# Two transformer networks in one f32 kernel: a fifth ring slot, transposed modulation sums, shifted low halves and a reordered feed-forward entry

## The chip, the cores and the metric

The kernel runs on one core of one Trainium2 chip. The metric is the device time of one execution in microseconds, as the median of the runs shown; lower is better. A profile is one such execution with the hardware profiler on.

## The reference

All tensors are f32; there are 256 tokens of width D = 2048. The first network has two layers, the second one adaLN block that takes a vector `c` of 2048 elements. Cut to what matters here:

```python
for l in range(2):                                   # first network
    proj = rmsnorm(x, norm_g[l]) @ w_in[l]           # 2048 x 7168
    y = concat([conv_branch, differential_attention, memory_attention])
    x = x + y @ w_out[l]

mod = silu(c) @ w_mod + b_mod                        # w_mod is 2048 x 12288
sh1, sc1, g1, sh2, sc2, g2 = split(mod, 6)
h = rms_norm(x, mix_norm_pre) * (1 + sc1) + sh1      # mixer
y = token_mixer(h)     # w_in_2, sliding-window attention, gated linear
                       # attention (GLA), two branch products, w_out_2
x = x + g1 * rms_norm(y, mix_norm_post)
h = rms_norm(x, ffn_norm_pre) * (1 + sc2) + sh2      # feed-forward block
u = causal_conv(h @ w_up)                            # 2048 x 11264
y = (silu(gate(u)) * val(u)) @ w_down                # 5632 x 2048
x = x + g2 * rms_norm(y, ffn_norm_post)
```

## The kernel before, in words

**Products.** Every large product is made in three passes of TensorE: an f32 operand is split into a high half (`hi`, a cast to fp32r) and a low half (`lo`, what the cast left), and the product is hi·hi + hi·lo + lo·hi. I call these three matmuls a *triple*. `gemm_as` (lines 342 to 356) and `gemm_halves` (360) hold the activations stationary and stream 512 weight columns; the rows of a triple stand in lines 354, 355 and 356. `gemm_ws` (393 to 408) holds the weights stationary and streams the 256 tokens; its lines are 406, 407 and 408. The split activations live in pairs of tiles: A (high) and B (low), or C (high) and D (low), 16 KB a partition each. `pair_AB` (1296) makes the pair A, B with the low half moved by 32 elements, 128 bytes, inside B; elsewhere A, B and C, D start where their tiles start.

**The weights' path.** The weights come as pieces of 512 KB (two tiles of 128 rows, 512 columns), in one fixed list of items. `load` (218) issues a piece on SP's queue into a slot of the ring `raw`, which has `RB` = 4 slots; `consume` (224) lets ScalarE cast it to `hi` and VectorE subtract to `lo`, into rings of `HB` = 4 slots. The load of the piece `RB` places on is issued by SP after `consume`, and waits for that slot:

```python
if j + self.RB < len(src):
    load(j + self.RB)
```

All other work (normalisations, attention, evacuations of PSUM, transposes) is written as Python generators. `run` (206) calls `tick` (278) after each piece, which advances these generators as far as a credit of VectorE and ScalarE time allows: first `evac`, then `urgent`, then background tasks. So the order on each engine is fixed when the program is built.

**The modulation.** `w_mod` has 192 pieces, which `spread_mod` (187) puts between the others: 64 in the first network, 96 in the mixer, 32 in the feed-forward block. `plan_mod` (596) turns each into two steps of VectorE, `macc = raw * c + macc`, 512 columns wide. After eight pieces `mod_done` (622) transposes `macc` in blocks of 32 and reduces it to `mred`; after four such groups a matmul with a matrix of ones sums `mred` over the partitions, and the result plus `b_mod` goes to `modT`.

**Second network.** `mixer` (1796) ends with the product with `w_out_2`; its last 512 columns run in `gemm_halves`, and `ev_last` (1931) then makes the residual rows X (`y` in the rows) of the first 128 tokens (tb 0) and the first chunk of the others (tb 1). `add_x` (1966) adds one chunk of 512 columns. `residual` (1975) does the rest chunk by chunk: `raw_chunk` (1315) transposes a chunk on TensorE, and between its steps stand the next chunk's `add_x`, the store of x and the sums of squares. `shift_norm` (1350) makes the pair C, D for the product with `w_up`; `ffn` (1998) makes the pair `gv` in A, B for the product with `w_down`, whose last 512 columns again run in `gemm_halves`.

Of the kernel before, what the change touches and what calls it, by code (L numbers as in the profile page):

```python
# [6 lines left out]
F32 = mybir.dt.float32  # L7
F32R = mybir.dt.float32r
# [3 lines left out]
ALU = mybir.AluOpType  # L12
AX = mybir.AxisListType

P = 128
# [45 lines left out]
    return [512] * (n // 512)  # L61


def row_tiles(n):

    return 16 if n == 16 else 1024 // n


def lay_pieces(np, name, w):

    layers, rows, n = w.shape
    out, c0 = np.empty((layers, rows * n), w.dtype), 0
# [81 lines left out]


class Kernel:
    RB = 4
    HB = 4
    NBG = 3
    CAP = 4.5  # L160
# [302 lines left out]
    def setup(self, ctx):  # L463
        nc, tc, a = self.nc, self.tc, self.a
        pool = lambda name, **k: ctx.enter_context(tc.tile_pool(name=name, bufs=1, **k))
        self.cp = pool("consts")
        self.wp = pool("weights")
        self.ap = pool("acts")
        dp = pool("dram", space=bass.MemoryType.DRAM)
        self.scr = {n: dp.tile(s, F32, tag=n, name=n) for n, s in (  # L470
            ("x1", [2 * P, D]), ("x2", [2 * P, D]), ("x3", [2 * P, D]), ("gp1", [D]), ("gp2", [D]))}
# [12 lines left out]
        self.mhalf = self.cp.tile([P, 16], F32, tag="mhalf", name="mhalf")  # L484
        self.cols = self.cp.tile([P, 704], F32, tag="cols", name="cols")
        self.modT = self.cp.tile([P, 96], F32, tag="modT", name="modT")
        raw = self.st["xraw"] = self.ap.tile([P, 16, 256], F32, tag="X16", name="xraw")
# [22 lines left out]
    def params(self):  # L510
# [22 lines left out]

        yield
        self.st["params"] = True

    def params_attn(self):
        nc, a = self.nc, self.a
# [56 lines left out]

    def plan_mod(self):

        nc = self.nc
        self.mod_queue = deque()
        w = self.weight("w_mod_2")  # L600
        for j in range(24):
            box = {}
            for k0 in range(0, 16, 2):
                def fn(raw, j=j, k0=k0, box=box):
                    if k0 == 0:
                        if j > 1:
                            self.await_tasks(f"red{j - 2}", bg=False)
                        box["acc"] = self.cp.tile([P, 512], F32, tag="macc", name=self.nm("macc"), bufs=2)
                    acc = box["acc"]
                    for kk in range(2):  # L610
                        s = self.ca[:, k0 + kk:k0 + kk + 1]
                        if k0 + kk == 0:
                            nc.vector.tensor_scalar(out=acc, in0=raw[:, kk], scalar1=s, scalar2=None, op0=ALU.mult)
                        else:
                            nc.vector.scalar_tensor_tensor(out=acc, in0=raw[:, kk], scalar=s, in1=acc,
                                                           op0=ALU.mult, op1=ALU.add)
                    if k0 == 14:
                        self.evac.append(self.mod_done(j, acc))
                src = w.piece(k0, 2, j * 512, 512)
                self.mod_queue.append(Item("mod", fn, src, 2, 512))  # L620

    def mod_done(self, j, acc):

        nc = self.nc
        yield
        if j % 4 == 0:
            self.mred = self.cp.tile([P, 64], F32, tag="mred", name=self.nm("mred"), bufs=2)
        red = self.mred
        while not self.t1.ok():
            yield  # L630
        for h in range(2):
            tr = self.t1.get()
            nc.vector.transpose(tr, acc[:, 256 * h:256 * h + 256])
            b = 16 * (j % 4) + 8 * h
            nc.vector.tensor_reduce(out=red[:, b:b + 8], in_=tr.rearrange("p (b i) -> p b i", i=32), axis=AX.X, op=ALU.add)
            self.t1.put(tr)
        self.st[f"red{j}"] = True
        if j % 4 < 3:
            return
        yield  # L640
        yield
        pt = self.bank()
        nc.side.matmul(pt[:, 0:64], self.cst[:, C_SUM:C_SUM + P], red, start=True, stop=True)
        for q in range(4):
            b = slice(32 * q, 32 * q + 32)
            nc.vector.tensor_tensor(out=self.modT[b, 4 * j - 12:4 * j + 4],
                                    in0=pt[b, 0:64].rearrange("p (c q) -> p q c", q=4)[:, q],
                                    in1=self.cols[b, R_BMOD + 4 * j - 12:R_BMOD + 4 * j + 4], op=ALU.add)
        self.ps.put(pt)
        for i in range(4):  # L650
            self.st[f"mod{j - i}"] = True

    def mod_row(self, gcol, postcol, dst):

# [237 lines left out]
    def layer(self, l, last):  # L892
# [137 lines left out]
        def out_begin():  # L1030
# [8 lines left out]
            if last:  # L1039
                self.await_tasks(*[f"mod{j}" for j in range(8)])  # L1040
                self.shifted("G1", R_MIXPRE, 16, 0)
                st["raw"] = [self.lp.tile([P, 4, 256], F32, tag=t, name=self.nm("raw")) for t in ("dv", "dg", "mkT", "mg")]
            else:
                st["xT2"] = [self.ap.tile([P, 16, 256], F32R, tag=t, name=self.nm(t)) for t in ("A", "B")]
# [305 lines left out]
    def shift_norm(self):  # L1350
# [15 lines left out]
        self.t1.put(dg)  # L1366
        self.ps.put(pt)
        st["r_ready"] = True
        hi, lo = [self.ap.tile([P, 16, 256], F32R, tag=t, name=self.nm(t)) for t in ("C", "D")]
# [241 lines left out]
    def gla_pair(self, c):  # L1611
# [5 lines left out]
        for hh in range(2):  # L1617
# [178 lines left out]
    def mixer(self):  # L1796
# [134 lines left out]
        def ev_last(acc):  # L1931
            c = slice(1536, 2048)
            X, ss, gp = st["X"], st["ss"], st["gp1"].pop(0)
            r = st["ry"] = self.sm.get([P, 2])
            for tb in range(2):
                rt = r[:, tb:tb + 1]
                self.square_sum(acc[tb], ss[:, tb, 3:4])
                nc.vector.tensor_reduce(out=rt, in_=ss[:, tb], axis=AX.X, op=ALU.add)
                self.rstd(rt, rt, 1.0 / D, 1)
                if tb == 0:  # L1940
                    nc.vector.tensor_tensor(out=X[:, tb, c], in0=acc[tb], in1=gp, op=ALU.mult)
                for n in range(1 if tb else 4):
                    self.add_x(n, tb)
            self.ps.put(acc[0])
            st["y"] = acc[1], gp
            yield
# [10 lines left out]
    def open_f(self):  # L1957
# [8 lines left out]
    def add_x(self, n, tb):  # L1966

        nc, st = self.nc, self.st
        xo, r = st[f"xo{n}"], st["ry"]
        x = st["X"][:, tb, n * 512:n * 512 + 512]  # L1970
        nc.vector.scalar_tensor_tensor(out=x, in0=x, scalar=r[:, tb:tb + 1], in1=xo[:, tb], op0=ALU.mult, op1=ALU.add)
        if tb:
            self.tm.put(st.pop(f"xo{n}"))

    def residual(self):
# [4 lines left out]
        for n in range(4):  # L1980
            c = slice(n * 512, n * 512 + 512)
            for i, _ in enumerate(self.raw_chunk(X[:, :, c], n, st["raw"][n])):
                if n == i == 0:
                    acc, gp = st.pop("y")
                    nc.vector.tensor_tensor(out=X[:, 1, 1536:2048], in0=acc, in1=gp, op=ALU.mult)
                    self.ps.put(acc)
                if i:
                    if n < 3:
                        self.add_x(n + 1, 1)
                    nc.sync.dma_start(out=self.scr["x3"][:, c].rearrange("(t p) d -> p t d", p=P), in_=X[:, :, c])  # L1990
                    for tb in range(2):
# [6 lines left out]
    def ffn(self):  # L1998
# [263 lines left out]
```

## Time and profile before

| | us |
|---|---|
| median of 3 runs (lowest, highest) | 2567.68 (2567.05, 2570.22) |
| the profiled execution, its own time | 2563.99 |
| its span, first to last instruction | 2562.2 |

The mean granted clock of TensorE in the profiled execution was 0.997 of full. Of the page, part 1 gives the busy time of each engine, part 5 groups of instructions, part 6 the DMA issues. Times of a stretch count from the span's start: the first network runs to 966 us, the mixer to 1710, its last output columns and the entry to the feed-forward block to 1850, then the products with `w_up` and `w_down` take turns in three parts each; the first part of `w_down` runs from 1985 to 2073 us, the second of `w_up` from 2073 to 2258. PE's waits name what TensorE waited for: `PE acc L355 <- DVE lo` is line 355 waiting for VectorE's `lo`.

### The profile page before, as it was taken

How to read it: one execution, taken by the hardware profiler on the slowest of the kernel's cores; microseconds unless marked ns; L12 is line 12 of the kernel's file. 1: busy time of each engine (PE TensorE's matmuls, PEld its weight loads, DVE VectorE, ACT ScalarE, POOL GpSimd, SP SyncE). 2: the span in 40 equal slices, each digit the busy share in tenths (PEclk: the TensorE clock that was granted, in tenths of full speed). 3: DMA queues.
4: the chain of work that ended last, by engine and by line, in shares of the span. 5: the costliest groups of instructions: out<-in, count | busy, mean ns of one | idle time of the engine just before them, and what ended most of it. 6: DMA issues, size and time to landing. Idle time of an engine off the chain costs nothing.

```text
span 2562.2 us, 38632 instructions
## 1 busy us (share of the span) xinstructions
PE 2526.8 (99%) x15079; PEld 2227.7 (87%) x15079; DVE 1823.1 (71%) x2469; ACT 1266.9 (49%) x1826; POOL 52.0 (2%) x43
## 2 busy tenths in 40 slices
PE   9999999999999999999999999999999999999998
PEld 7889998788899989878988778777999899988996
DVE  6768767786786756777777777775777667765665
ACT  6645544564554455355454334344744444543443
POOL 1000000010010000000000000000000000000000
PEclk9999999999999999999999999999999999999999
DMA  8775568887656576755558888886566766676655
GB/s 311 225 255 181 179 197 271 299 272 256 220 179 190 180 249 187 224 173 190 193 182 267 285 290 286 280 289 210 164 215 231 230 215 214 223 236 197 198 188 174
DMA packets 168903, 576.77 MB, mean 225 GB/s; under 512 B 18272, under 2 KB 24576, under 8 KB 168720
## 3 DMA queue, kind: packets, MB, share of 16 engines
q1 hardware_dynamic: 168432, 574.04, 69.0%
q8 instruction: 118, 1.93, 0.3%
q14 instruction: 65, 0.53, 0.1%
q10 hardware_dynamic: 288, 0.26, 0.0%
HBM read 565.83 MB, written 8.40 MB: 224 GB/s over the span
## 4 chain that ended last, share of the span: by engine, by line
PE 77%; DMA 9%; DVE 8%; ACT 3%; issue 2%; POOL 0%; ACTq 0%; DVEq 0%; POOLq 0%
PE acc L355 13%; PE acc L356 13%; PE acc L354 13%; PE acc L406 10%; PE acc L407 10%; PE acc L408 10%; PE pb L133 5%; DMA raw<-w_in 4%; DVE lo L133 4%; ACT hi L133 2%; DMA raw<-w_out 2%; DMA raw<-w_branch_gla 1%; DVE macc L133 1%; DMA raw<-w_branch_attn 1%; DVE tm L133 1%
## 5 line engine op out<-in xcount | busy, mean ns | idle before, releaser
L133 DVE TENSOR_TENSOR lo<-raw,hi 128x1024 fp32r<-128x1024 f32 (+1 forms) x847 | 1026.8, 1220 | 515.7 <-ACT hi L133 511.2
L133 ACT CAST hi<-raw 128x1024 fp32r<-128x1024 f32 (+1 forms) x847 | 881.7, 1048 | 867.6 <-PE acc L356 281.4
L408 PE MATMUL acc<-C,lo 128*128 128x256 f32 (+1 forms) x1424 | 403.0, 283 | 0.8 <-DVE lo L133 0.8
L406 PE MATMUL acc<-C,hi 128*128 128x256 f32 (+1 forms) x1424 | 403.7, 284 | 0.0
L407 PE MATMUL acc<-D,hi 128*128 128x256 f32 (+1 forms) x1424 | 402.9, 283 | 0.0
L354 PE MATMUL acc<-hi,C 128*128 128x512 f32 x992 | 393.1, 396 | 0.0
L355 PE MATMUL acc<-lo,C 128*128 128x512 f32 x992 | 387.4, 390 | 4.0 <-DVE lo L133 3.9
L356 PE MATMUL acc<-hi,D 128*128 128x512 f32 x992 | 387.0, 390 | 0.0
L355 PE MATMUL acc<-lo,A 128*128 128x512 f32 x904 | 357.7, 396 | 1.2 <-DVE lo L133 1.1
L356 PE MATMUL acc<-hi,B 128*128 128x512 f32 x904 | 357.9, 396 | 0.0
L354 PE MATMUL acc<-hi,A 128*128 128x512 f32 x904 | 354.2, 392 | 0.7 <-ACT hi L133 0.7
L133 DVE SCALAR_TENSOR_TENSOR macc<-raw,ca,macc 128x512 f32<-128x512 f32 x360 | 269.7, 749 | 9.9 <-DMA raw<-w_mod 2.9
L406 PEld LDWEIGHTS acc<-C,hi 128*128 128x128 f32 (+1 forms) x1424 | 271.7, 191 | 1.5 <-issue 0.7
L408 PEld LDWEIGHTS acc<-C,lo 128*128 128x128 f32 (+1 forms) x1424 | 271.7, 191 | 1.4 <-DVE lo L133 1.0
L407 PEld LDWEIGHTS acc<-D,hi 128*128 128x128 f32 (+1 forms) x1424 | 271.8, 191 | 0.6
L406 PE MATMUL acc<-A,hi 128*128 128x256 f32 x896 | 256.3, 286 | 0.0
L407 PE MATMUL acc<-B,hi 128*128 128x256 f32 x896 | 252.0, 281 | 0.0
L408 PE MATMUL acc<-A,lo 128*128 128x256 f32 x896 | 251.2, 280 | 0.3 <-DVE lo L133 0.2
L355 PEld LDWEIGHTS acc<-lo,C 128*128 128x128 f32 x992 | 186.4, 188 | 45.5 <-DVE lo L133 7.9
L354 PEld LDWEIGHTS acc<-hi,C 128*128 128x128 f32 x992 | 186.3, 188 | 40.5 <-issue 3.4
L356 PEld LDWEIGHTS acc<-hi,D 128*128 128x128 f32 x992 | 186.2, 188 | 39.3
L354 PEld LDWEIGHTS acc<-hi,A 128*128 128x128 f32 x904 | 172.7, 191 | 40.9 <-ACT hi L133 1.6
(269 smaller groups left out, 2989.5 us busy)
## 6 DMA issues: line engine op xcount, KB each, us to landing
raw<-w_in SPq DMA_DIRECT2D x406, 512.0 KB, 4.4
raw<-w_mod SPq DMA_DIRECT2D x192, 512.0 KB, 4.6
raw<-w_up SPq DMA_DIRECT2D x176, 512.0 KB, 4.2
raw<-w_out SPq DMA_DIRECT2D x96, 512.0 KB, 4.5
raw<-w_down SPq DMA_DIRECT2D x88, 512.0 KB, 4.3
raw<-w_mem_kv SPq DMA_DIRECT2D x32, 512.0 KB, 4.4
raw<-w_branch_gla SPq DMA_DIRECT2D x32, 512.0 KB, 4.7
tm<-x SPq DMA_DIRECT2D x20, 512.0 KB, 6.2
```

The costliest lines, as they stand in the source:

```text
L133: return f(*args, **kw)
L354: nc.tensor.matmul(o, xh[:, kt, t], hi, start=s, stop=False)
L355: nc.tensor.matmul(o, xh[:, kt, t], lo, start=False, stop=False)
L356: nc.tensor.matmul(o, xl[:, kt, t], hi, start=False, stop=e)
L406: nc.tensor.matmul(o, hi[:, c], xh, start=s and j % 2 == 0, stop=False, skip_group_check=True)
L407: nc.tensor.matmul(o, hi[:, c], xl, start=False, stop=False, skip_group_check=True)
L408: nc.tensor.matmul(o, lo[:, c], xh, start=False, stop=e, skip_group_check=True)
```

## The change

1. `RB` goes from 4 to 5.
2. `w_mod` is laid out transposed: a piece holds 128 output columns on the partitions and one half (1024) of the inputs along the row. One custom VectorE instruction per piece multiplies it with a broadcast row of silu(c) (`crow`, one half of 1024 at a time) and sums into `mpart` (first half) or, with `mpart` added, into `modT`. `macc`, `mred`, `mod_done` and its matmuls are gone; `b_mod` is added once in four pieces of a second half. The groups (0,8), (8,20), (20,24) set when the half changes; `crow` is broadcast six times, and a sum of the new half waits for its broadcast.
3. The low half D is allocated 64 elements longer and moved by `skew`: 0 in the mixer, 32 elements in the feed-forward block. `gv` uses `pair_AB`.
4. `ev_last` sums the squares of tb 0 itself (ScalarE) and three quarters of tb 1's sum ahead of the last, merges the last steps into one, and adds the first chunk of tb 1 in two halves of 256 columns. `residual` adds each chunk of tb 1 one step earlier, and squares tb 1 alone but in the last chunk.
5. `gla_pair` writes two gates in place of q and k (`V` tiles 6 to 4). The extra slot and the rows `crow` and `mpart` move every later tile in SBUF.

```diff
-    RB = 4
+    RB = 5
...
+        for i, (h, b) in enumerate(order):
+            def fn(raw, i=i, h=h, b=b):
+                self.await_tasks(f"crow{self.mod_half[i]}", bg=False)
+                d = raw.rearrange("p k n -> p (k n)")
+                out = self.mpart[:, b:b + 1] if h == 0 else self.modT[:, b:b + 1]
+                nc.vector.tensor_tensor_reduce(out=d, in0=d, in1=self.crow, scale=1.0,
+                                               scalar=0.0 if h == 0 else self.mpart[:, b:b + 1], op0=ALU.mult, op1=ALU.add,
+                                               accum_out=out)
...
+                if i + 1 < len(order) and self.mod_half[i + 1] != self.mod_half[i]:
+                    self.evac.append(self.crow_load(self.mod_half[i + 1]))
...
+    def crow_load(self, m):
+
+        for _ in range(2 if m else 0):
+            yield
+        h = m % 2
+        self.nc.sync.dma_start(out=self.crow, in_=self.scr["crow"][1024 * h:1024 * h + 1024].partition_broadcast(P))
+        self.st[f"crow{m}"] = True
...
+        lo = self.ap.tile([P, 16 * 256 + 64], F32R, tag="D", name=self.nm("D"))
+        s = st["skew"]
+        lo = lo[:, s:s + 4096].rearrange("p (k t) -> p k t", t=256)
...
-            Q, K, QI, KS, K2, QD = V(0), V(1), V(2), V(3), V(4, (2, P)), V(5, (2, 64))
+            Q, K, QI, KS, K2, QD = V(0), V(1), q, k, V(2, (2, P)), V(3, (2, 64))
...
+            nc.vector.tensor_reduce(out=r1, in_=ss[:, 1, 0:3], axis=AX.X, op=ALU.add)
+            nc.vector.tensor_scalar(out=r1, in0=r1, scalar1=1.0 / D, scalar2=EPS, op0=ALU.mult, op1=ALU.add)
+            for n in range(4):
+                self.add_x(n, 0)
+                if n < 3:
+                    self.square_sum(X[:, 0, n * 512:n * 512 + 512], ss[:, 0, n:n + 1])
+            self.square_sum(acc[1], ss[:, 1, 3:4])
+            nc.vector.scalar_tensor_tensor(out=r1, in0=ss[:, 1, 3:4], scalar=1.0 / D, in1=r1, op0=ALU.mult, op1=ALU.add)
+            nc.gpsimd.tensor_tensor(out=r1, in0=r1, in1=self.mhalf[:, :1], op=ALU.pow)
+            for i in range(2):
+                self.add_x(0, 1, i)
...
                 if n == i == 0:
                     acc, gp = st.pop("y")
+                    self.add_x(1, 1)
                     nc.vector.tensor_tensor(out=X[:, 1, 1536:2048], in0=acc, in1=gp, op=ALU.mult)
                     self.ps.put(acc)
+                if (n, i) in ((0, 1), (1, 0)):
+                    self.add_x(2 + n, 1)
                 if i:
-                    if n < 3:
-                        self.add_x(n + 1, 1)
                     nc.sync.dma_start(out=self.scr["x3"][:, c].rearrange("(t p) d -> p t d", p=P), in_=X[:, :, c])
-                    for tb in range(2):
+                    for tb in range(0 if n == 3 else 1, 2):
                         self.square_sum(X[:, tb, c], ss[:, tb, n:n + 1])
...
-                st["gv"] = [self.ap.tile([P, 16, 256], F32R, tag=t, name=self.nm(t)) for t in ("A", "B")]
+                st["gv"] = self.pair_AB()
```

What this does to the order on the engines, at three places. VectorE before, in the feed-forward block, around one modulation piece that ends a group of eight (`tm` are steps of the convolution, `t1k` the transposed blocks):

```order
L133 TENSOR_TENSOR lo_18289<-raw_18157,hi_18288 128x1024
L133 SCALAR_TENSOR_TENSOR macc_17168<-raw_18196,ca,macc_17168 128x512 x2
L133 TENSOR_TENSOR lo_18323<-raw_18231,hi_18322 128x1024
L133 TENSOR_TENSOR lo_18353<-raw_18261,hi_18352 128x1024
L133 STREAM_TRANSPOSE t1k_82_18383<-macc_17168 128x256
L133 TENSOR_REDUCE mred_18382<-t1k_82_18383 128x8
```

VectorE now, in the mixer near its first branch product, with three pieces (`ISA` is the custom sum, and behind it the read of the accumulator; `ml` is an evacuation):

```order
L145 ISA raw_13497,mpart<-raw_13497,crow 128x1024
L145 ISA mpart 128x1
L145 TENSOR_TENSOR lo_13586<-raw_13521,hi_13585 128x1024
L145 ISA raw_13537,modT<-raw_13537,crow,mpart 128x1024
L145 ISA modT 128x1
L145 TENSOR_TENSOR lo_13608<-raw_13543,hi_13607 128x1024
L145 TENSOR_TENSOR lo_13628<-raw_13567,hi_13627 128x1024
L145 ISA raw_13583,modT<-raw_13583,crow,mpart 128x1024
```

Per piece one long step stands between the `lo` steps where two stood, and nothing is left to do after eight pieces. SP's queue now, at the same place, where the half changes:

```order
L234 DMA raw_13537<-w_mod 128x1024
L234 DMA raw_13543<-w_branch_attn 128x1024
L234 DMA raw_13567<-w_branch_attn 128x1024
L234 DMA raw_13583<-w_mod 128x1024
L234 DMA raw_13589<-w_in 128x1024
L646 DMA crow<-crow 128x1024
L234 DMA raw_13605<-w_in 128x1024
L234 DMA raw_13611<-w_mod 128x1024
```

The broadcast has come in between the weight loads; here, as at one other of the six places, the sum that needs it is that of a piece loaded just ahead of it (`raw_13537`, the first into `modT`), and on VectorE the rows behind that sum stand behind the broadcast.

VectorE before, at the entry to the feed-forward block (`y` is X, `tm` the chunks of x, `B` the low half of `raw_chunk`):

```order
L133 TENSOR_REDUCE sm_117_16149<-sm_116_15503 128x1
L133 TENSOR_SCALAR sm_117_16149<-sm_117_16149 128x1
L133 SCALAR_TENSOR_TENSOR y_15502<-y_15502,sm_117_16149,tm_65_15528 128x512
L133 SCALAR_TENSOR_TENSOR B_16006<-pb_217_16172,G_16003,A_16005 128x256 x2
L133 TENSOR_TENSOR y_15502<-pb_216_16016,gpr_4_15853 128x512
L133 SCALAR_TENSOR_TENSOR B_16006<-pb_218_16184,G_16003,A_16005 128x256 x2
L133 SCALAR_TENSOR_TENSOR y_15502<-y_15502,sm_117_16149,tm_66_15646 128x512
```

And now:

```order
L145 SCALAR_TENSOR_TENSOR sm_117_15842<-sm_116_15209,sm_117_15842 128x1
L145 SCALAR_TENSOR_TENSOR y_15208<-y_15208,sm_117_15842,tm_65_15234 128x256 x2
L145 SCALAR_TENSOR_TENSOR B_15699<-pb_213_15870,G_15696,A_15698 128x256 x2
L145 SCALAR_TENSOR_TENSOR y_15208<-y_15208,sm_117_15842,tm_66_15350 128x512
L145 TENSOR_TENSOR y_15208<-pb_212_15709,gpr_4_15546 128x512
L145 SCALAR_TENSOR_TENSOR B_15699<-pb_214_15883,G_15696,A_15698 128x256 x2
L145 SCALAR_TENSOR_TENSOR y_15208<-y_15208,sm_117_15842,tm_67_15431 128x512
```

Two steps on the sum became one, the first chunk is added in halves, and the chunks `tm_66` and `tm_67` are added one step earlier against the `B` rows of the chunk before.

## Rows read from the trace of the kernel before

**Rows 1.** Page, part 1: busy time of each engine in the whole span

```profile
PE 2526.8 (99%) x15079; PEld 2227.7 (87%) x15079; DVE 1823.1 (71%) x2469; ACT 1266.9 (49%) x1826; POOL 52.0 (2%) x43
```

**Rows 2.** Windows by stage: length, busy time (instructions) by engine, PEclk, DMA, GB/s

```profile
0.00:966.00 966.00, 961.86 (x5698) 845.43 (x5699) 699.15 (x963) 516.06 (x803) 42.92 (x29) 1.00 0.72 231
966.00:1710.00 744.00, 732.04 (x3755) 609.11 (x3754) 563.59 (x804) 345.09 (x494) 5.44 (x9) 1.00 0.73 237
...
1710.00:1782.00 72.00, 68.67 (x296) 56.41 (x297) 41.96 (x47) 33.60 (x44) 0.28 (x1) 0.98 0.73 242
1782.00:1850.00 68.00, 61.67 (x464) 59.58 (x463) 50.70 (x90) 49.10 (x104) 1.53 (x3) 0.95 0.46 146
...
1850.00:2562.20 712.20, 702.59 (x4873) 657.14 (x4871) 467.66 (x570) 323.02 (x382) 1.84 (x2) 1.00 0.65 211
```

**Rows 3.** Waits of PE in the mixer, 966 to 1710 us: total, times, longest

```profile
PE acc L355 <- DVE lo L133: 5.9, 12, 0.9
...
PE pb L133 <- DVE tm L133: 4.2, 3, 2.1
```

**Rows 4.** Waits of PE, 1710 to 1785 us, then 1782 to 1850 us

```profile
PE pb L133 <- DVE mred L133: 3.3, 1, 3.3
...
PE pb L133 <- DVE y L133: 4.5, 2, 2.5
```

**Rows 5.** Timeline near 1443 us: start, us, engine, operation, [idle before, ended by]

```profile
1441.75 1.53 DVE L133 SCALAR_TENSOR_TENSOR macc<-raw,ca,macc 128x512 f32<-128x512 f32 x2
...
1443.83 1.05 ACT L133 CAST hi<-raw 128x1024 fp32r<-128x1024 f32 x1 [3.25 <-DMA raw<-w_in]
...
1446.19 0.50 PE L355 MATMUL acc<-lo,C 128*128 128x512 f32 x1 [0.77 <-DVE lo L133]
```

**Rows 6.** Waits of ACT in the mixer, 966 to 1710 us

```profile
ACT hi L133 <- DMA raw<-w_in: 114.9, 63, 4.1
```

**Rows 7.** DMA issues, KB each, median us to landing

```profile
raw<-w_in SPq DMA_DIRECT2D x406, 512.0 KB, 4.4
...
gpr<-gp SPq DMA_DIRECT2D x8, 256.0 KB, 5.7
```

**Rows 8.** Line 354 in three stretches: ns of one (min/median/max), first and last start

```profile
L354 PE MATMUL acc<-hi,A x128: 389/389/396, 1984.9 to 2073.0; 128*128 128x512 f32 x128
...
L354 PE MATMUL acc<-hi,C x52: 389/389/389, 121.4 to 156.0; 128*128 128x512 f32 x52
...
L354 PE MATMUL acc<-hi,A x32: 389/389/398, 1503.7 to 1524.9; 128*128 128x512 f32 x32
```

**Rows 9.** Line 406 in three stretches

```profile
L406 PE MATMUL acc<-C,hi x512: 277/283/283, 2073.7 to 2257.6; 128*128 128x256 f32 x171
...
L406 PE MATMUL acc<-A,hi x105: 274/282/469, 326.7 to 363.6; 128*128 128x256 f32 x105
...
L406 PE MATMUL acc<-A,hi x64: 278/279/282, 846.2 to 868.2; 128*128 128x256 f32 x64
```

**Rows 10.** Groups of DVE by form: busy us, mean ns | idle before

```profile
L133 DVE TENSOR_TENSOR lo<-raw,hi 128x1024 fp32r<-128x1024 f32 x842 | 1023.7, 1223 | 515.3 <-ACT hi L133 510.8
...
L133 DVE SCALAR_TENSOR_TENSOR macc<-raw,ca,macc 128x512 f32<-128x512 f32 x360 | 269.7, 749 | 9.9 <-DMA raw<-w_mod 2.9
...
L133 DVE STREAM_TRANSPOSE t1k<-macc 128x256 f32<-128x256 f32 x48 | 20.9, 436 | 0.1
...
L133 DVE TENSOR_REDUCE mred<-t1k 128x8 f32<-128x256 f32 x48 | 20.2, 420 | 1.7
```

**Rows 11.** The same view of ACT

```profile
L133 ACT ACTIVATION_READ_ACCUMULATOR e2k<-e2k,sm 128x1 f32 x80 | 15.2, 190 | 0.0
```

**Rows 12.** Groups of PE in the mixer, 966 to 1710 us

```profile
L354 PE MATMUL acc<-hi,C 128*128 128x512 f32 x609 | 242.3, 398 | 0.0
```

**Rows 13.** Timeline at the feed-forward entry

```profile
1788.56 0.98 PE L133 MATMUL pb<-cst,y 128*128 128x128 f32 x7 [2.53 <-DVE y L133]
...
1801.01 0.76 PE L133 MATMUL pb<-cst,y 128*128 128x128 f32 x3 [2.00 <-DVE y L133]
```

More of the change, by code (lines that the diff above doesn't have):

```diff
@@ L61, in cuts, with mod_order @@
     return [512] * (n // 512)
+MOD_GROUPS = ((0, 8), (8, 20), (20, 24))
+def mod_order():
+    return [(h, b) for j0, j1 in MOD_GROUPS for h in range(2) for b in range(4 * j0, 4 * j1)]
 def row_tiles(n):
@@ L71, in lay_pieces @@
     layers, rows, n = w.shape
+    if name == "w_mod_2":
+        half = [w[:, 1024 * h:1024 * h + 1024, P * b:P * b + P].transpose(0, 2, 1) for h, b in mod_order()]
+        return np.stack(half, 1).reshape(layers, rows * n)
     out, c0 = np.empty((layers, rows * n), w.dtype), 0
@@ L470, in setup @@
         self.scr = {n: dp.tile(s, F32, tag=n, name=n) for n, s in (
-            ("x1", [2 * P, D]), ("x2", [2 * P, D]), ("x3", [2 * P, D]), ("gp1", [D]), ("gp2", [D]))}
+            ("x1", [2 * P, D]), ("x2", [2 * P, D]), ("x3", [2 * P, D]), ("gp1", [D]), ("gp2", [D]), ("crow", [D]))}
         self.psA = ctx.enter_context(tc.tile_pool(name="psA", bufs=2, space=bass.MemoryType.PSUM))
@@ L486, in setup @@
         self.modT = self.cp.tile([P, 96], F32, tag="modT", name="modT")
+        self.mpart = self.cp.tile([P, 96], F32, tag="mpart", name="mpart")
+        self.crow = self.cp.tile([P, 1024], F32, tag="crow", name="crow")
         raw = self.st["xraw"] = self.ap.tile([P, 16, 256], F32, tag="X16", name="xraw")
@@ L535, in params @@
         self.st["params"] = True
+        for _ in range(6):
+            yield
+        yield from self.c_row()
     def params_attn(self):
@@ L599, in plan_mod @@
         self.mod_queue = deque()
[L600 to L620, printed above, removed]
@@ L622, in mod_done @@
-    def mod_done(self, j, acc):
-        nc = self.nc
-        yield
[L626 to L639, printed above, removed]
+        order = mod_order()
@@ new lines, in plan_mod @@
+        for i, (h, b) in enumerate(order):
[6 more added lines that the diff above has]
+                                               accum_out=out)
+                if h and b % 4 == 3:
+                    j = b // 4
+                    nc.vector.tensor_tensor(out=self.modT[:, b - 3:b + 1], in0=self.modT[:, b - 3:b + 1],
+                                            in1=self.col(R_BMOD + b - 3, 4), op=ALU.add)
+                    self.st[f"mod{j}"] = True
+                if i + 1 < len(order) and self.mod_half[i + 1] != self.mod_half[i]:
+                    self.evac.append(self.crow_load(self.mod_half[i + 1]))
+            src = self.a["w_mod_2"][0][i * P * 1024:(i + 1) * P * 1024].rearrange("(p k n) -> p k n", p=P, k=2)
+            self.mod_queue.append(Item("mod", fn, src, 2, 512))
@@ new lines, in plan_mod, with c_row @@
+        self.mod_half, m = [], -1
+        for i, (h, b) in enumerate(order):
+            m += i == 0 or h != order[i - 1][0]
+            self.mod_half.append(m)
+    def crow_load(self, m):
+        for _ in range(2 if m else 0):
+            yield
+        h = m % 2
+        self.nc.sync.dma_start(out=self.crow, in_=self.scr["crow"][1024 * h:1024 * h + 1024].partition_broadcast(P))
+        self.st[f"crow{m}"] = True
+    def c_row(self):
+        nc = self.nc
+        pt = self.bank()
+        self.transpose(pt[:16, :P], self.ca)
+        row = self.t1.get([P, 256])
+        nc.vector.tensor_copy(row[:16, :P], pt[:16, :P])
+        self.ps.put(pt)
+        yield
+        nc.sync.dma_start(out=self.scr["crow"].rearrange("(k p) -> k p", p=P), in_=row[:16, :P])
+        self.t1.put(row)
@@ L640, in mod_done @@
         yield
         yield
[L642 to L648, printed above, removed]
@@ L649, in mod_done @@
-        self.ps.put(pt)
-        for i in range(4):
-            self.st[f"mod{j - i}"] = True
+        yield from self.crow_load(0)
     def mod_row(self, gcol, postcol, dst):
@@ L1041, in out_begin @@
                 self.shifted("G1", R_MIXPRE, 16, 0)
+                st["skew"] = 0
                 st["raw"] = [self.lp.tile([P, 4, 256], F32, tag=t, name=self.nm("raw")) for t in ("dv", "dg", "mkT", "mg")]
@@ L1368, in shift_norm @@
         st["r_ready"] = True
-        hi, lo = [self.ap.tile([P, 16, 256], F32R, tag=t, name=self.nm(t)) for t in ("C", "D")]
+        hi = self.ap.tile([P, 16, 256], F32R, tag="C", name=self.nm("C"))
+        lo = self.ap.tile([P, 16 * 256 + 64], F32R, tag="D", name=self.nm("D"))
+        s = st["skew"]
+        lo = lo[:, s:s + 4096].rearrange("p (k t) -> p k t", t=256)
         st["hT"] = (hi, lo)
@@ L1934, in ev_last @@
             r = st["ry"] = self.sm.get([P, 2])
-            for tb in range(2):
[L1936 to L1943, printed above, removed]
+            r0, r1 = r[:, 0:1], r[:, 1:2]
+            self.square_sum(acc[0], ss[:, 0, 3:4])
+            nc.vector.tensor_reduce(out=r0, in_=ss[:, 0], axis=AX.X, op=ALU.add)
+            self.rstd(r0, r0, 1.0 / D, 1)
+            nc.vector.tensor_tensor(out=X[:, 0, c], in0=acc[0], in1=gp, op=ALU.mult)
+            nc.vector.tensor_reduce(out=r1, in_=ss[:, 1, 0:3], axis=AX.X, op=ALU.add)
[9 more added lines that the diff above has]
+                self.add_x(0, 1, i)
             self.ps.put(acc[0])
@@ L1964, in open_f, with add_x @@
         self.st["h_ready"] = self.st["r_ready"] = self.st["u_done"] = False
-    def add_x(self, n, tb):
+        self.st["skew"] = 32
+    def add_x(self, n, tb, half=None):
         nc, st = self.nc, self.st
         xo, r = st[f"xo{n}"], st["ry"]
-        x = st["X"][:, tb, n * 512:n * 512 + 512]
-        nc.vector.scalar_tensor_tensor(out=x, in0=x, scalar=r[:, tb:tb + 1], in1=xo[:, tb], op0=ALU.mult, op1=ALU.add)
-        if tb:
+        s = slice(0, 512) if half is None else slice(256 * half, 256 * half + 256)
+        x = st["X"][:, tb, n * 512:n * 512 + 512][:, s]
+        nc.vector.scalar_tensor_tensor(out=x, in0=x, scalar=r[:, tb:tb + 1], in1=xo[:, tb, s], op0=ALU.mult, op1=ALU.add)
+        if tb and half != 0:
             self.tm.put(st.pop(f"xo{n}"))
```

1 line of the change is left out of this document (removed).

## Prediction

> **What bounds the kernel now.** I read the page's busy table first: TensorE is busy in nearly the whole span [rows 1]. "Busy" there includes waiting weight loads and modelled ends, so I asked the trace for two finer things: how fast matmuls follow each other where nothing disturbs them, and where TensorE sat idle. The stage table [rows 2] shows the idle time (window less PE busy): 12.0 us in the second network's mixer (966 to 1710 us), 3.3 us in its output product, 6.3 us at the entry to the feed-forward block, and 9.6 us from 1850 us on, nearly all of it the chain after the last matmul, which the change leaves alone. All of it comes to 35 us. So the change can win in two ways only: by removing those waits, or by letting matmuls follow each other faster. DVE, at 76% in the mixer, and the DMA engines, at 73%, bound nothing on average; they end waits one at a time.
>
> Who ends the waits: in the mixer mostly the low halves of the weights and results that VectorE hands to transposes [rows 3]; in the output product a single reduction of the modulation vector, and at the entry the residual rows y [rows 4]. One wait followed back [rows 5]: TensorE waits 0.77 us for `lo`, `lo` for ScalarE's cast, and that cast for its weight tile, which came 3.25 us after ScalarE was free. Between them stand two modulation steps on VectorE, 1.53 us. Over the mixer, ScalarE waits 115 us for tiles of the second `w_in` alone, in 63 waits [rows 6]. A tile lands about 4.4 us after its issue [rows 7], and its slot is given back only when VectorE is done with it. The ring of four runs dry whenever VectorE falls behind.
>
> **The change, part by part**, against the profiled execution's own 2564.0 us; the median of the three runs, 2567.7 us, is 3.7 us above it.
>
> *Addresses.* In the down product a triple of matmuls (both halves of an operand) starts every 693.7 ns (128 triples, 1984.9 to 2073.0 us). The same loop takes 678 ns with the tiles C and D, and 684 ns with A and B where `pair_AB` already shifts the low half by 128 bytes; that window holds some bubbles, so I take 682 [rows 8]. The change puts `pair_AB` under the whole down product: 328 triples and 24 in its last chunk, 352 x 11.7 ns = 4.1 us. The up product streams C and D at 359.9 ns a triple; where the first network streams A and B, whose halves lie 128 bytes off a multiple of 16 KB, it is 354.8 ns in one stretch and 349 in another [rows 9]. The shift of `lo` by 32 elements (`skew`) gives the up product the same distance. I take 353 ns: 1,280 triples x 6.9 ns = 8.8 us; the ends are 5.1 and 10.9 ns, or 6.5 to 14 us. Together 12.9 us.
> [...]
>
> *Modulation sums.* Each 512 KB piece of `w_mod` costs VectorE two steps of 749 ns now, and its share of 48 transposes and 48 reductions (436 and 420 ns, over 192 pieces 0.21 us) [rows 10]: 1.71 us. After it is one custom multiply-and-sum over 1024 elements and a read of the accumulator. No row has that operation. Lower bound: the plain two-input step of that shape, 1.22 us; upper bound: the two steps it replaces, 1.50 us. I take 1.25, nearest to the row of the same shape, with 0.19 us for the read as on ScalarE [rows 11]: 1.44 us. That is 0.27 us less, 192 times: 52 us of VectorE, 26 of them in the mixer. It lies beside TensorE, so it counts only where VectorE ends a wait.
> [...]
>
> *Waits.* The 3.3 us wait for `mred` and its matmuls go with the code: 3.9 us with the 0.2 us in the mixer and six matmul pairs. Of the other 11 us of mixer waits I let the fifth slot and the shorter VectorE queue remove 8. A fifth slot moves each load's issue one piece, 2.7 us or more, earlier, against tiles that are 3.2 us late in the example. Bounds: 0 and 11. Matmuls in the mixer are also stretched by waits too short to be idle time: 609 have a mean of 398 ns [rows 12] against the undisturbed 389 in rows 8, so 5.5 us; I take 3.
>
> *Entry to the feed-forward block.* TensorE waits 2.53 us for the first rows y and 2.00 us for those of the third chunk, whose residual stands behind the chunk before [rows 13]. Half a residual (about 0.27 us less) and a merged sum (0.2 us) shorten the first. The second goes, since that residual now stands a chunk ahead. With small change from the squares moved into ScalarE's idle time: 3 of 6.3 us; bounds 1 and 5.
>
> *What it adds.* Six broadcasts of the row c. Two of them, as the order rows on SP show, stand behind the load of the piece four places on, so they are issued only as VectorE reaches the sum that needs them. A 256 KB broadcast of the same sort lands after 5.7 us [rows 7]; VectorE, and every `lo` and result behind that sum, waits so long. TensorE has up to three prepared pieces of 2.7 us in hand: between 0 and 4 us for each, I take 1. At the start the prefix loop with the larger ring loads the last 256 KB of x twice, 1.1 us at the 231 GB/s of the first 966 us [rows 2]: I take 1. The in-place gates of the linear attention, the squares and the stores stay the same in number and size and lie beside TensorE's matmuls; where that cover is missing, before the first rows y, their moves are in the entry's term.
>
> **Sum:** -12.9 - 3.9 - 8 - 3 - 3 + 3 = -27.8 us. So 2536.2 us for a profiled execution, **2540 us** for the median.
>
> **Rivals.**
> 1. *The ring does not starve, VectorE's order does.* Then the mixer keeps its 11 us (waits and stretch), and the broadcasts take 3 us more: 2554 us. For it: some mixer waits end on VectorE results, not on `lo`. Against: rows 5 and 6. Chance 0.14.
> 2. *Placement gives nothing.* The pools before the activations also change size, so all tiles lie some 3.9 KB higher; if the absolute address counts and not the distance, the 12.9 us are not there: 2553 us. Rows 8 and 9 favour distance, since C and D, equally placed in both products, are fast as one operand and slow as the other. Chance 0.10.
> 3. [...] Chance 0.08.
> 4. *The shift hurts:* every triple of 512 columns slows by the 13 ns between the good and the bad pair, 2,056 of them, 27 us: 2567 us, no change. Chance 0.03.
>
> **Numbers.** The forecast has 0.65; its own range is 2529 to 2552 us (the bounds above, not all at once). The range 2527 to 2561 takes in rivals 1 and 2 and leaves out 3, 4 and the tails. A difference of 0.2%, 5 us, is about what a measurement can tell from no change. Faster: the forecast and rivals 1 and 2, less the case that both hold: 0.86. Same 0.06, slower 0.08.
>
> **What would show it.** Right: in the down product triples at 680 to 684 ns, in the up product at 349 to 355; a sum step of 1.2 to 1.3 us; no `mred`; ScalarE's waits for tiles in the mixer well under 115 us, and PE idle there about 4 us; at the entry one wait near 2 us and no second. Wrong: a sum step over 2 us; mixer waits as long as now with tiles in time; triples at 693 and 360; a wait of several us on TensorE at the second or fourth broadcast.

## The result and the profile after

The changed kernel takes 2524.4 us (2523.13 to 2524.88, 4 runs) against 2567.36 us for the kernel before: a ratio of 0.983, 95% interval 0.982 to 0.985. I had forecast 2540 us and a range from 2527; the gain is real, half as large again as I worked out, and the time lies outside the range. The profiled execution took 2524.62 us, so the two profiled executions differ by 39.4 us. One of the eleven executions of sumonly, below, took 2737.82 us at a mean granted clock of 0.849, where the others have 0.994 to 0.997, and is left out of its figures.

Page of the changed kernel, part 1, busy time of each engine (before: rows 1):

```profile
PE 2502.8 (99%) x15068; PEld 2216.8 (88%) x15068; DVE 1747.9 (69%) x2376; ACT 1264.8 (50%) x1826; POOL 53.7 (2%) x43
```

VectorE has 75 us less to do, TensorE's busy time falls by 24 us though it makes almost the same matmuls: the gain is partly matmuls that follow each other faster. Windows of the changed kernel, cut where each stage begins (columns as in rows 2): first network, mixer, output product, feed-forward entry, the rest:

```profile
0.00:965.80 965.80, 963.26 (x5698) 847.51 (x5699) 674.67 (x932) 514.77 (x803) 44.59 (x29) 1.00 0.71 233
965.80:1675.00 709.20, 706.38 (x3665) 594.86 (x3664) 517.45 (x749) 339.82 (x488) 5.42 (x9) 1.00 0.72 242
1675.00:1766.40 91.40, 89.23 (x401) 73.53 (x399) 54.56 (x61) 42.11 (x59) 1.10 (x2) 1.00 0.75 257
1766.40:1820.40 54.00, 51.36 (x411) 50.80 (x412) 43.71 (x76) 44.35 (x93) 0.70 (x1) 0.97 0.54 168
1820.40:2522.80 702.40, 692.57 (x4899) 650.11 (x4897) 457.53 (x559) 323.74 (x385) 1.84 (x2) 1.00 0.65 214
```

In the mixer TensorE is idle for 2.8 us where it was 12.0. (Rows 2 count the first 20 us of the output product to the mixer; cut at the same matmul, 1692.9 us, the changed kernel still has 2.8.) Waits of TensorE there, 966 to 1695 us (total, times, longest), the whole view, to set beside rows 3:

```profile
PE pb L145 <- DVE gA L145: 1.5, 1, 1.5
PE acc L367 <- DVE lo L145: 0.8, 1, 0.8
PE acc L440 <- DVE X L145: 0.6, 1, 0.6
```

and ScalarE's wait for the same tiles as in rows 6, 966 to 1690 us, 25 us where it was 115:

```profile
ACT hi L145 <- DMA raw<-w_in: 24.6, 11, 5.3
```

The two products of the feed-forward block, one line of a triple each (columns as in rows 8):

```profile
L366 PE MATMUL acc<-hi,A x128: 389/389/394, 1956.0 to 2042.4; 128*128 128x512 f32 x128
L418 PE MATMUL acc<-C,hi x512: 274/282/283, 2043.1 to 2223.6; 128*128 128x256 f32 x171
```

127 intervals in 86.4 us and 511 in 180.5 us: triples of 680 ns in the down product (693 before) and 353 ns in the up product (360 before) [rows 8, 9].

Every run makes the same 14064 large matmuls in the same order, so I read from each trace when the first of a stage starts, and take the differences. Here the output product begins with its first matmul, 1689 us before, and not at 1710 as in rows 2. This table (us, one profiled execution of each kernel, in the order of the program) also holds the experiments that follow:

| kernel | first network | mixer | output product | entry | up, 3 parts | down and end |
|---|---|---|---|---|---|---|
| before | 966.9 | 722.6 | 100.2 | 56.0 | 461.9 | 254.6 |
| changed | 965.8 | 709.1 | 91.5 | 53.9 | 452.4 | 250.1 |
| changed, second trace (again) | 963.8 | 708.6 | 91.5 | 52.3 | 453.5 | 250.1 |
| ring5only | 964.6 | 709.2 | 92.2 | 55.2 | 461.9 | 254.5 |
| ring4 | 972.7 | 717.0 | 95.5 | 52.4 | 452.2 | 250.2 |
| ring4bothhalves | 967.0 | 712.3 | 96.0 | 53.9 | 452.4 | 250.1 |
| sumonly | 972.9 | 720.1 | 96.0 | 55.9 | 461.9 | 254.5 |
| oldsum | 965.9 | 709.2 | 91.7 | 52.4 | 451.5 | 250.3 |
| oldsum2 (oldsum again) | 965.1 | 709.2 | 91.7 | 52.4 | 451.5 | 250.3 |
| noplace | 964.2 | 709.5 | 91.5 | 52.4 | 462.0 | 254.4 |
| placeonly | 968.5 | 721.4 | 99.7 | 56.0 | 452.7 | 250.4 |
| oldentry | 966.1 | 708.6 | 92.3 | 54.5 | 452.2 | 250.1 |
| skewmixer | 964.7 | 714.1 | 91.5 | 52.4 | 453.5 | 250.1 |
| normearly | 965.5 | 709.2 | 91.8 | 51.6 | 451.4 | 250.3 |

So of the 39.4 us the first network gave 1.1, the mixer 13.5, the output product 8.7, the entry 2.1, the up product 9.5 and the down product with the end 4.5. Two executions of the same kernel (changed, again) differ by up to 2 us in the first network and 1.6 in the entry, so less than that in one of these columns proves nothing.

### The profile page after: what moved, and what is told of

It reads as the page before. It is cut to its first block, busy times and chain, and to the rows that moved or that the text cites. A ratio compares the mean times of both kernels' runs of the same rounds, so it can differ in the third digit from the quotient of the medians.

```text
span 2522.8 us, 38530 instructions
## 1 busy us (share of the span) xinstructions
PE 2502.8 (99%) x15068; PEld 2216.8 (88%) x15068; DVE 1747.9 (69%) x2376; ACT 1264.8 (50%) x1826; POOL 53.7 (2%) x43
## 5 line engine op out<-in xcount | busy, mean ns | idle before, releaser
L419 PEld LDWEIGHTS acc<-D,hi 128*128 128x128 f32 (+1 forms) x1424 | 266.3, 187 | 0.6
L367 PEld LDWEIGHTS acc<-lo,A 128*128 128x128 f32 x904 | 170.2, 188 | 37.1 <-DVE lo L145 0.8
```

The costliest lines, as they stand in the source:

```text
L367: nc.tensor.matmul(o, xh[:, kt, t], lo, start=False, stop=False)
L419: nc.tensor.matmul(o, hi[:, c], xl, start=False, stop=False, skip_group_check=True)
```

## The experiments

My theory: placement makes the up and down products faster; the starved ring of four is the cause of the waits in the mixer and of most in the output product. The main rival: VectorE's shorter queue is what counts. The kernel before was run again with each set: its median was 2563.6 us beside ring4, oldsum, noplace and oldentry, 2564.0 beside again, ring5only, ring4bothhalves and placeonly, and 2565.6 beside skewmixer, sumonly, oldsum2 and normearly. The changed kernel itself (again) ran in the second set: 2523.46 us.

**ring4**: the changed kernel with four slots.

```diff
-    RB = 5
+    RB = 4
```

> The changed kernel with four ring slots again (RB = 4), all else as changed. Theory (the ring starved and the fifth slot cured it): most of the 13.4 us that the mixer gained come back, so 2532 to 2538 us, with waits of ScalarE for weight tiles in the mixer near 100 us again. Rival (the shorter VectorE queue was what counted, because a slot is given back when VectorE is done with it): 2524 to 2528 us.

2543.69 us (ratio to before 0.993, 0.991 to 0.994): some 20 us slower than with five slots, more than either theory allowed. Waits of VectorE for the broadcast rows in the whole trace:

```profile
DVE raw L145 <- DMA crow<-crow: 12.9, 2, 6.6
```

and what one of them does (timeline; in brackets the idle time before, and what ended it):

```profile
1479.62 1.28 DVE L145 CUSTOM_DVE_ANT_0 raw<-raw,crow,mpart 128x1024 f32<-128x1024 f32 x1 [6.59 <-DMA crow<-crow]
...
1482.10 0.80 PE L367 MATMUL acc<-lo,oaT 128*128 128x512 f32 x1 [4.41 <-DVE lo L145]
```

VectorE waits 6.6 us for the row, the low half behind it is late, TensorE stands for 4.4 us, and the next matmul takes 0.80 us where 0.39 is usual. Windows of 5 us show why (the column before the last two is the granted clock):

```profile
1477.00:1482.00 5.00, 0.70 (x4) 0.24 (x2) 2.38 (x4) 1.07 (x2) 0.00 (x0) 0.95 0.32 112
1482.00:1487.00 5.00, 4.90 (x12) 3.84 (x13) 3.61 (x5) 1.26 (x2) 0.00 (x0) 0.50 0.89 287
1487.00:1492.00 5.00, 5.00 (x21) 4.05 (x20) 3.52 (x4) 2.71 (x3) 0.00 (x0) 0.87 0.90 318
```

Behind the wait the clock is at 0.50 for 5 us and at 0.87 in the next 5. From these two clocks I estimate that 2.5 + 0.65 us more are lost than the idle time shows. ScalarE's wait for tiles of `w_in` in the mixer is 118.6 us again. The four-slot run mixes two prices, so the next run takes them apart.

**ring4bothhalves**: four slots, with both halves of the row kept (the slot's room holds the second).

```diff
-    self.crow = self.cp.tile([P, 1024], F32, tag="crow", name="crow")
+    self.crow = self.cp.tile([P, 2048], F32, tag="crow", name="crow")
...
-                self.await_tasks(f"crow{self.mod_half[i]}", bg=False)
+                self.await_tasks("crow0", bg=False)
```

> The changed kernel with four ring slots, and both halves of the row silu(c) kept in SBUF in the room that the slot leaves, so that no broadcast is waited for after the first two. Theory (19 us of the four-slot run are two prices: about 11 us for two waits for broadcasts, which four slots can't cover, and the starved ring): 2531 to 2535 us. Rival (all of it is the ring, the broadcasts cost nothing): 2541 to 2545 us.

2533.01 us (0.988, 0.987 to 0.989), as the theory had it: the two broadcasts cost 10.7 us with four slots (by the table 5.7 in the first network, 4.7 in the mixer), and the missing slot itself 9.6 us against the changed kernel (2523.46 in the same set). ScalarE still waits for tiles as long as before:

```profile
ACT hi L145 <- DMA raw<-w_in: 114.2, 64, 5.1
```

Yet the mixer takes 712.3 us where it took 722.6 before: ScalarE's wait is a sign that the ring runs dry, but no measure of what TensorE loses by it.

**ring5only**: the kernel before with the fifth slot and the two in-place gates that make its room.

```diff
-    RB = 4
+    RB = 5
...
-            Q, K, QI, KS, K2, QD = V(0), V(1), V(2), V(3), V(4, (2, P)), V(5, (2, 64))
+            Q, K, QI, KS, K2, QD = V(0), V(1), q, k, V(2, (2, P)), V(3, (2, 64))
```

> The kernel before with five ring slots alone (and the two gates of the linear attention written in place, which make the room). Theory (four slots starve, and the wait for mred and the clock dip behind it are of the same cause): the mixer's 13 us and the output product's 8 us both go, 2541 to 2545 us against 2564 to 2567 before. Rival (the ring needs the new sums or the new addresses to pay): 2553 us or more, with the wait for mred still near 3 us.

2539.34 us (0.990, 0.989 to 0.992), 24.6 us less than before and more than the theory gave: by far the largest part, and in the table the mixer and the output product are within 1 us of the changed kernel's. The in-place gates alone don't do it: ring4 and ring4bothhalves keep them, and their ScalarE waits for tiles are back. TensorE's waits from 966 to 1770 us, with the old sums in place:

```profile
PE pb L133 <- DVE y L133: 2.5, 1, 2.5
PE acc L355 <- DVE lo L133: 0.9, 1, 0.9
PE pb L133 <- DVE gA L133: 0.8, 1, 0.8
PE acc L428 <- DVE X L133: 0.6, 1, 0.6
PE acc L429 <- DVE B L133: 0.3, 1, 0.3
```

ScalarE waits 19.5 us for tiles of `w_in`. TensorE's wait for `mred` [rows 4] is not in the list, though `mred` is still computed. It was a sign of the starved ring, not a property of the sum.

**oldsum**: the changed kernel with the sums of before (`plan_mod`, `mod_done`, the plain layout of `w_mod`; one `mred` buffer in place of two). Its edit is the modulation part of the change, undone.

> The changed kernel with the modulation sums of before (two steps into macc, mred, the matmul with ones; one mred buffer in place of two, for room), all else as changed. Theory: the wait for mred in the output product and the clock dip behind it come back, 3.5 + 1.7 us, and in the mixer little, since five slots cover it: 2529 to 2532 us. Rival (VectorE's queue is what counts): the mixer's 13 us come back as well, 2538 to 2543 us.

2523.35 us (0.984, 0.983 to 0.986), and 2522.79 in the third set (oldsum2, the same kernel): the changed kernel's time. Both theories expected a loss, and both are wrong. With five slots the new sums and their broadcasts together bring nothing, though they free 75 us of VectorE.

**sumonly**: the kernel before with the new sums alone.

> The kernel before with the new modulation sums alone (row silu(c) broadcast six times), four ring slots. Theory (the shorter sum relieves the starved ring by some 16 us, two broadcasts that four slots can't cover take 11 back): 2556 to 2561 us. Rival (the sum does nothing for a kernel bound by TensorE): 2570 us or more, by the broadcasts' 11 us.

2562.42 us in the median of ten executions (0.9986, 0.9977 to 0.9995): 3.1 us less than before, just above what the theory gave, and the rival's loss is not there. By the table the sums win back 2.5 us in the mixer and 4.2 in the output product, and the first network is 6 us longer. In its trace VectorE waits 12.4 us for two broadcasts, one of them there. With four slots a shorter VectorE queue does help, once the broadcasts are out of its way (ring4bothhalves: the mixer at 712.3 us against 722.6), but it cures what the fifth slot cures too.

**noplace** and **placeonly**: the changed kernel without the shifts, and the kernel before with the shifts alone (one `mred` buffer, for room).

```diff
-        lo = self.ap.tile([P, 16 * 256 + 64], F32R, tag="D", name=self.nm("D"))
-        s = st["skew"]
-        lo = lo[:, s:s + 4096].rearrange("p (k t) -> p k t", t=256)
+        hi, lo = [self.ap.tile([P, 16, 256], F32R, tag=t, name=self.nm(t)) for t in ("C", "D")]
...
-                st["gv"] = self.pair_AB()
+                st["gv"] = [self.ap.tile([P, 16, 256], F32R, tag=t, name=self.nm(t)) for t in ("A", "B")]
```

> The changed kernel without the shift of the low halves (D not shifted, gv as plain tiles A and B), all else as changed. Theory (distance of the two halves): the 9.5 us of the up product and the 4.6 us of the down product come back, 2537 to 2540 us, up triples at 360 ns, down triples at 694 ns. Rival (it was the higher absolute address of all tiles): 2524 us, and the triples stay as fast as in the changed kernel.

> The kernel before with the shift of the low halves alone (one mred buffer in place of two, for room). Theory (distance): up triples at 352 to 354 ns and down triples at 680 to 682 ns, 14 us less than before, 2550 to 2553 us, with the waits of the mixer as before. Rival (absolute address): no change, 2562 to 2567 us.

noplace 2536.88 us (0.990, 0.989 to 0.991), 13.4 us above the changed kernel of the second set; placeonly 2552.75 us (0.995, 0.994 to 0.997), 11.2 us below before. One-line view of the up product in noplace, 360 ns a triple again (183.6 us for 510) although all tiles lie as high as in the changed kernel, to 256 bytes:

```profile
L418 PE MATMUL acc<-C,hi x511: 283/283/283, 2045.9 to 2229.5; 128*128 128x256 f32 x171
```

and in placeonly, 353 ns (180.5 us for 511) with the tiles of before:

```profile
L406 PE MATMUL acc<-C,hi x512: 274/282/283, 2069.4 to 2249.9; 128*128 128x256 f32 x171
```

Here the distance counts (353 ns with the shift, 360 without) and the absolute address doesn't, and the effect is about the same alone and on top of the others (11.2 and 13.4 us).

**skewmixer**: the shift in the mixer too.

```diff
-                st["skew"] = 0
+                st["skew"] = 32
```

> The changed kernel with the low half D shifted by 32 elements in the mixer too, where the change leaves it at 0. Theory (a product with stationary activations wants both halves at the same distance, one that streams them wants 128 bytes between): 610 triples of the mixer that hold C and D stationary slow by 11 to 12 ns each, 7 us, 128 triples that stream C and D gain 7 ns, 1 us: 2528 to 2531 us. Rival (a shift always helps or never matters): 2518 to 2524 us.

2528.34 us (0.986, 0.984 to 0.987), 4.9 us above the changed kernel of the second set, and the mixer 5.5 us longer by the table. One stretch of 32 triples that hold C and D stationary in skewmixer, 693 ns each (21.5 us for 31):

```profile
L366 PE MATMUL acc<-hi,C x32: 389/389/389, 1400.6 to 1422.1; 128*128 128x512 f32 x32
```

and in the changed kernel's second trace, 680 ns (from the starts to the nanosecond; the row's rounded ones give 677):

```profile
L366 PE MATMUL acc<-hi,C x32: 389/389/390, 1396.9 to 1417.9; 128*128 128x512 f32 x32
```

So 128 bytes more between C and D went with faster triples where they are the moving operand (360 to 353 ns) and with slower ones where they are the stationary one (680 to 693). But the same 128 bytes sped `gv` in A and B, which is stationary too, from 693 to 680 ns. The two pairs start from different distances: A and B also hold tiles of 258 columns, 16 x 258 x 4 = 16512 bytes, so they lie 128 bytes more than 16 KB apart, and 256 with `pair_AB`; C and D lie 16 KB apart. Triples by that distance:

| beyond 16 KB | stationary, 512 columns streamed | moving, 256 columns |
|---|---|---|
| 0 bytes | 680 ns (C, D in the mixer) | 360 (C, D before) |
| 128 | 693 (A, B before; C, D in skewmixer) | 353 (C, D shifted) |
| 256 | 680 (A, B with `pair_AB`) | no run |

This expectation's theory, the same distance for a stationary pair, is thus too narrow: 256 bytes do as well as none.

**oldentry**: the changed kernel with `ev_last`, `add_x` and `residual` of before.

> The changed kernel with the entry to the feed-forward block in the order of before (squares, whole first residual, residuals behind the chunk), all else as changed. Theory: the second wait for y (2.2 us) and a second dip of the clock (1.7 us) come back, the new wait for the normalisation (2.3 us) goes: 2526 to 2528 us. Rival (the new wait takes all that the old one gave): 2524 us.

2526.21 us (0.986, 0.984 to 0.987) against 2523.46 in the second set: about 2.7 us, as the theory had it, but too near to the scatter to tell the two theories apart by time. The waits tell them apart: TensorE's waits in oldentry, whole trace, against the changed kernel's between 1675 and 1821 us:

```profile
PE pb L145 <- DVE y L145: 4.2, 2, 2.5
```

```profile
PE pb L145 <- DVE t1k L145: 2.1, 1, 2.1
PE pb L145 <- DVE y L145: 2.1, 1, 2.1
PE acc L441 <- DVE B L145: 0.5, 1, 0.5
```

One wait for the rows y went, and a wait of the same length for the normalisation's diagonal blocks (`t1k`) came.

**normearly** (oldsum2 is its base): the reduction and these blocks directly behind the last squares.

```diff
-                        self.evac.append(self.shift_norm())
+                        self.evac.append(self.shift_norm(self.norm_head()))
```

> The changed kernel with the modulation sums of before, and the last step of the residual changed: the reduction of the squares and the two diagonal blocks of the normalisation stand right behind the last squares instead of one tick later, behind a low half that waits for ScalarE. Theory (the wait of 2.1 us for the normalisation is order alone): that wait goes, 2519 to 2522 us, some 2 to 3 us less than the run beside it. Rival (the low half, now later, stops TensorE instead): no difference.

2522.6 us (0.9835, 0.982 to 0.985), oldsum2 2522.79: no difference that can be told. The wait for `t1k` is gone from its trace. But in oldsum2 it was only 0.8 us (2.1 in oldsum), and by the table the entry is 0.8 us shorter. The theory's 2 to 3 us were read from one trace, and that wait varies: oldsum2 has a window at 0.67 of the clock from 1765 to 1770 us, oldsum none, and the entry takes 52.4 us in both. I read it so that what the low clock took there, the shorter wait gave back. This kernel is as fast as the changed one, with the simpler old sums; it does not beat it measurably.

> The changed kernel itself, unaltered, beside the others of this set, so that a few microseconds can be compared on the same chip. Both theories: 2520 to 2525 us.

again: 2523.46 us (0.984, 0.983 to 0.986).

## Why the prediction was wrong, point by point

To set my terms against the result I cut the changed kernel at the same matmuls as rows 2 cut the kernel before. The profiled execution gained 1.1 us in the first 966 us, 16.2 in the mixer as I had cut it (to 1710 us), 5.5 in the output product (to 1782), 3.6 at the entry (to 1850) and 13.0 behind it.

- **Addresses, -12.9 us: right.** 13.0 us went from 1850 us on; triples of 353 and 680 ns where I took 353 and 682. noplace and placeonly measure 13.4 and 11.2 us for it. Which distance is good depends on the operand (skewmixer: 128 bytes more, 693 ns stationary for 680, while the moving pair has 353 for 360); why it matters stays open.
- **The price of the new sum: nearly right; its worth: wrong.** Its groups by form on VectorE:

```profile
L145 DVE CUSTOM_DVE_ANT_0 raw<-raw,crow,mpart 128x1024 f32<-128x1024 f32 x96 | 122.8, 1279 | 13.2 <-issue 6.4 <-DMA crow<-crow 6.3 <-DMA raw<-w_mod 0.4
...
L145 DVE CUSTOM_DVE_ANT_0 raw<-raw,crow 128x1024 f32<-128x1024 f32 x96 | 116.9, 1217 | 1.1 <-DMA raw<-w_mod 1.0
...
L145 DVE DVE_READ_ACCUMULATOR2_ANT mpart<- 128x1 f32 x96 | 7.9, 83 | 0.0
```

  1.33 us a piece where I took 1.44. 1.22 us is the time of the same shape without an accumulator [rows 10]; the custom step takes 1.22 us, and 1.28 where it adds `mpart`. But I booked the 3.3 us wait for `mred` as going "with the code". ring5only and oldsum keep the code and lose the wait.
- **The mixer: the step that failed most.** I forecast 10.2 us: 8 of 11 us of waits, 3 of 5.5 us of stretch and 0.2 of `mred`'s wait, less 1 for a broadcast. 16.2 us went. The mechanism was right: rows 5 and 6 read as a starved ring, and ring5only gives 16.2 us here by itself. The sizes were wrong. Of 12.0 us of idle time 9.2 went. The stretch I misread: the row that I took it from [rows 12] is the same in the changed kernel,

```profile
L366 PE MATMUL acc<-hi,C 128*128 128x512 f32 x608 | 242.0, 398 | 0.0
```

  so its 398 ns do not tell of waits, and 5.5 us were no bound. The other 7.0 us lie between the starts of matmuls: one is recorded for 389 ns, but the next starts 227 ns after it where nothing disturbs (a third of 680), so of each wait up to 162 ns do not show as idle time. That this is all of the 7.0 us is not shown.
- **The output product: the clock had no term.** I priced 3.7 us there; 5.5 went. The wait for `mred` was followed by a stretch at low clock, windows of the kernel before:

```profile
1710.00:1715.00 5.00, 2.45 (x10) 1.65 (x10) 4.93 (x8) 2.93 (x4) 0.00 (x0) 1.00 0.80 229
1715.00:1720.00 5.00, 4.22 (x12) 3.42 (x13) 3.64 (x8) 1.05 (x1) 0.00 (x0) 0.66 0.96 376
1720.00:1725.00 5.00, 5.00 (x23) 4.13 (x22) 2.87 (x3) 3.37 (x6) 0.00 (x0) 1.00 0.42 157
```

  12 matmuls where the next 5 us have 23: from the clock of 0.66 over 5 us I estimate 1.7 us lost behind the wait. The changed kernel's windows show 1.00 through this product. I had the 0.98 and 0.95 of rows 2 before me and gave the clock no term. (The table's 8.7 us for this product take in the 20 us before 1710, with 1.6 us of waits for `lo` and `tm`, and the first wait for y.)
- **What it adds, +3 us: wrong for five slots.** The first network is not longer, and of the two late broadcasts one stops TensorE for 0.8 us (the `lo` wait above), the other not at all. With four slots they cost 10.7 us. I priced the wait on VectorE against TensorE's reserve of before, and did not let the new slot enlarge that reserve.
- **The entry, -3 us: 3.6 measured, in part by luck.** Idle time fell only from 6.3 to 4.8 us: the second wait for y went, and behind it stands a new one of 2.1 us for `t1k`, which I had not named. The rest is mostly the clock, again without a term of mine: by the same estimate 3.4 us lost in two windows before,

```profile
1790.00:1795.00 5.00, 4.50 (x25) 4.44 (x25) 3.01 (x6) 3.44 (x9) 0.00 (x0) 0.66 0.18 65
...
1800.00:1805.00 5.00, 3.99 (x21) 4.00 (x22) 3.94 (x6) 4.90 (x10) 0.00 (x0) 0.66 0.47 156
```

  and 1.7 in the changed kernel:

```profile
1790.00:1795.00 5.00, 2.90 (x13) 2.54 (x12) 3.88 (x9) 2.23 (x4) 0.70 (x1) 0.74 0.75 241
1795.00:1800.00 5.00, 5.00 (x41) 5.00 (x40) 4.01 (x9) 2.46 (x8) 0.00 (x0) 0.92 0.58 197
```

- **From profile to median, +3.7 us: wrong.** I carried the distance of one profiled execution of before to a kernel whose profile (2524.62) and median (2524.4) agree.

Together: 6.0 us in the mixer, 3.1 in the first network, 1.8 in the output product, 0.6 at the entry and 0.1 behind it are the 11.6 us between 2536.2 and 2524.6; the 3.7 us come on top. Of the rivals, the first (VectorE's order, not the ring) falls with ring5only, the second (placement) with noplace, the third, the slower outcome with its chance of 0.08, with the rows above: no run shows a slower sum, it took 1.33 us a piece where 1.71 stood before. The fourth (the shift hurts) is true only of C and D held stationary, as skewmixer shows; the change does not shift them there.

## What to carry to other kernels

When several waits look alike (a late low half, a late reduction, a late result), ask which one resource feeds them all before pricing each with the code that it names: here one more slot of 512 KB removed most of them (ring5only, 24.6 us less), and a 75 us shorter VectorE queue then added nothing. A wait of a few microseconds on TensorE cost more than its length here: I estimate 1.7 us behind the wait for `mred` (3.3 us, clock 0.66) and 3.2 us behind one of 4.4 us (ring4, clock 0.50); in oldsum2, as I read it, a shorter wait behind the low clock gave it back. A mean duration above the undisturbed one (398 ns to 389) was no proof of waiting here; look for the same row where the waits are gone. The broadcasts, all but harmless with five slots (0.8 us on TensorE), cost 10.7 us with four, so price additions together with the reserve that covers them.

## What the runs showed of the hardware

- The pace of a triple went with the distance of the two tiles used in turn for one operand: as the moving operand 360 ns at 16 KB (before, noplace) and 353 at 128 bytes more (changed, placeonly); as the stationary operand 680 ns at 16 KB (again), 693 at 128 bytes more (before, skewmixer) and 680 at 256 more (changed). A row of the first matmul of a triple hides it (389 ns in the down product of both kernels, rows 8 for before); the third shows it, before and then changed:

```profile
L356 PE MATMUL acc<-hi,B x127: 395/397/397, 1985.4 to 2072.7; 128*128 128x512 f32 x127
```

```profile
L368 PE MATMUL acc<-hi,B x128: 389/389/389, 1956.5 to 2042.9; 128*128 128x512 f32 x128
```

  In the up product the weight loads show it, 192 ns before and 188 now:

```profile
L406 PEld LDWEIGHTS acc<-C,hi x512: 192/192/192, 2073.4 to 2257.5; 128*128 128x128 f32 x171
```

```profile
L418 PEld LDWEIGHTS acc<-C,hi x512: 187/188/190, 2042.9 to 2223.5; 128*128 128x128 f32 x171
```

- After an idle stretch of 4.4 us (ring4) TensorE's granted clock was 0.50 in the 5 us from 1482 us and 0.87 in the next 5. After the waits of some 2 us at the entry the clock dips in some executions and not in others: with the same two waits of 2.1 us the changed kernel's first trace shows 0.97 there, its second and that of oldsum 1.00.
- The broadcast of the row (512 KB by its issue row) landed after 5.8 us in the median of six in the changed kernel, where I had used 5.7 us from those of 256 KB [rows 7].
